# SwiGLU gate and up projections by seven block products in a two-layer encoder kernel

## The chip, the core and the metric

The kernel runs on one core of a Trainium2 chip, in one launch. The metric is the device time in microseconds. TensorE (PE) multiplies, VectorE (DVE) and ScalarE (ACT) do the elementwise work, GpSimd (POOL) a few sums, and SyncE (SP) issues nearly all transfers.

## The reference

Two layers; each has a SwiGLU, a mixer with three branches, and a second SwiGLU. Only the SwiGLUs' inner products change here. All data are float32; T = 512 tokens, D = 1024, F = 2816.

```python
def swiglu(h, w_gate, w_up, w_down):
    return (jax.nn.silu(h @ w_gate) * (h @ w_up)) @ w_down

c_act = jax.nn.silu(c)
for l in range(DEPTH):                       # 2
    mod = (c_act @ w_ada[l] + b_ada[l]).reshape(B, N_MOD, D_MODEL)       # 9 rows of 1024
    h = modulate(rms_norm(x, norm_gain[l, 0]), mod[:, 0], mod[:, 1])
    x = x + 0.5 * mod[:, 2][:, None, :] * swiglu(h, ffn_w_gate[l, 0], ffn_w_up[l, 0], ffn_w_down[l, 0])
    h = modulate(rms_norm(x, norm_gain[l, 1]), mod[:, 3], mod[:, 4])
    x = x + mod[:, 5][:, None, :] * hybrid_mixer(h, ...)
    h = modulate(rms_norm(x, norm_gain[l, 2]), mod[:, 6], mod[:, 7])
    x = x + 0.5 * mod[:, 8][:, None, :] * swiglu(h, ffn_w_gate[l, 1], ffn_w_up[l, 1], ffn_w_down[l, 1])
```

## The kernel before

Activations lie transposed, features on partitions and the 512 tokens along the columns. Every float32 product is made of three matmuls (`triple`, L117): an operand is split into a high part, rounded to fp32r, and a low part, the rest; hi x hi, hi x lo and lo x hi are added up in PSUM. The normalised input of a sub-layer is kept as `hhi` and `hlo`, eight blocks of 128 features by 512 tokens each. `pe` (L85) counts TensorE's work, in matmuls of 512 columns; `later` puts a piece of work behind a given count, and `poll` in `triple` runs what is due.

A weight chunk comes through `wchunk` (L243): a transfer of 512 KB into `raw` (two buffers), a cast on ScalarE to `whi` (L268), a subtraction on VectorE to `wlo` (L270), three buffers each. `wchunk` also fetches rows of w_ada: inside a SwiGLU, one per chunk (`MOD_RATE`), through `mod_pop` and `mod_step` (L191), which loads 512 KB into a `v2` buffer and makes the dot product with silu(c) on VectorE (L197). `mod_need` runs those rows at once that must be there by a given point.

A SwiGLU (`Ffn.run`, L461) goes in two parts, of 12 and 10 tiles of 128 hidden features. In each part, gate and up of one tile are made by eight triples each (`unit`, L447) into two `mm` banks; `act` (L452) makes silu on ScalarE, the product on VectorE in an SBUF tile `t2`, and the split into a block `b`. Then `k_outer` (L374) multiplies the part's tiles by w_down, in two halves of 512 output features: chunks of two tiles each, four accumulators of the `acc` tag, the last two chunks held back so that the accumulators end one after another. `residual_tail` (L416) adds each to x on VectorE (L420). The last half of a SwiGLU is done in two column halves of 256 tokens, so that the next norm can begin. The first tiles of a SwiGLU follow the norm in column halves too (L472 to L489); the very first SwiGLU has a start of its own (`start`, L523), which does three tiles of gate and up as the inputs arrive.

PSUM has two tags of four banks, `acc` and `mm`. SBUF tags that matter: `b` (17 blocks of 4 KB a partition), `v2` (4), `raw` (2), `whi` and `wlo` (3 each), `ptb` (2), `pta` (1), `strip` (2), `ssum` (1). The order of instructions on each engine is settled when the program is built, mainly by the order in the source; on the chip each engine takes its own in order.

Of the kernel before, what the change touches and what calls it, by code (L numbers as in the profile page):

```python
# [40 lines left out]
def encoder_kernel(tc, xT, c, w_ada, b_ada, gains, w_gate, w_up, w_down, w_qkv, w_f, w_ubg,  # L41
# [75 lines left out]
    def triple(o, lh, ll, rh, rl, start, stop):  # L117
        poll()
        mm(o, lh, rh, start=start, stop=False)  # L119
        mm(o, lh, rl, start=False, stop=False)  # L120
        mm(o, ll, rh, start=False, stop=stop)  # L121
        pe[0] += 3.0 * max(o.shape[-1], 256) / T
# [103 lines left out]
    MOD_RATE = 1.0  # L226
# [16 lines left out]
    def wchunk(src, shape, side=True, spare=None, lo_eng=None):  # L243
# [3 lines left out]
        if quiet[0] > 0:  # L247
            quiet[0] -= 1
            if quiet[0] == 0:
                gate.clear()  # L250
        elif side and in_ffn[0] and mod_tag[0] == "v2":
            mod_credit[0] += MOD_RATE
            while mod_credit[0] >= 1.0:
                mod_credit[0] -= 1.0
                mod_pop()
        raw = st([P] + list(shape), F32, *(("b", NB) if spare else ("raw", NRAW)))
# [37 lines left out]
    class Norm:  # L294


        def __init__(self, l, s, xtag):
# [5 lines left out]
            self.pieces = [[], []]  # L303

# [39 lines left out]
        def back_start(self, hs, bank):  # L344
# [9 lines left out]
            def piece(d):  # L354
# [8 lines left out]
                last["norm"] = v_ins.ins  # L363

# [9 lines left out]
    def k_outer(chunk_src, nch, lhs_rhs, before_last=None):  # L374
# [3 lines left out]
        if before_last is None:  # L378
            parts, nheld = [(None, slice(0, T), [acc() for _ in range(4)])], 2
# [14 lines left out]
        for c in range(nch):  # L394
# [34 lines left out]
    STEP = 3  # L429


    class Ffn:
# [19 lines left out]
        def act(self, n, pg, pu):  # L452
            sg = t1(T)
            nc.scalar.activation(sg, pg, AF.Silu)
            pr = t2(T)
            nc.vector.tensor_tensor(pr, pu, sg, op=ALU.mult)  # L456
            a = blk("b")
            split_to(a[:, 0, :], a[:, 1, :], pr)
            return a

        def run(self, nxt):  # L461
# [3 lines left out]
            for part, (f0, nf) in enumerate(((0, 12), (12, 10))):  # L465
                acts = []
                n = 0
                if part == 0 and self.norm is None:
                    acts = self.start()
                    n = 3  # L470
                elif part == 0:
                    g0, u0, g1 = self.pre  # L472
                    pg, pu, pg1 = mmt(), mmt(), mmt()
# [10 lines left out]
                    u1 = self.gate_up(1, 1)  # L484
# [4 lines left out]
                    n = 2  # L489
# [601 lines left out]
```

## Time and profile before

| | |
|---|---|
| time, three runs | 2480.24 us median, 2478.81 to 2480.90 |
| span of the profiled execution | 2478.9 us (its time is told by this span alone) |
| TensorE busy, matmuls | 2425.1 us (98%), 11898 |
| VectorE busy | 1372.2 us (55%) |
| ScalarE busy | 979.9 us (40%) |
| GpSimd busy | 340.5 us (14%) |
| transfers | 320.02 MB, 129 GB/s on average |
| the four SwiGLUs, about | 15 to 388, 888 to 1240, 1240 to 1628, 2128 to 2479 us |

In the profile's rows, L12 is line 12 of the kernel; PE is TensorE's matmuls and PEld its weight loads. A group's row has its count, its busy time in us and the mean of one in ns, then the idle time of its engine just before it and what ended that. A tile's or line's row has minimum, median and maximum in ns. A timeline's row begins with start and duration in us. A window's row has for each engine the busy time and, in brackets, the instructions; then the granted clock of TensorE, the share of the transfer engines and GB/s. Matmuls overlap, so the step from one start to the next tells what one costs.

### The profile page before, as it was taken

The page shows a single profiled execution, that of the slowest core. Times are in us where ns is not written, and L with a number is a line of the kernel's source. Part 1 is how long each engine was busy: PE and PEld are TensorE (multiplying, and loading weights), DVE is VectorE, ACT ScalarE, POOL GpSimd, SP SyncE. Part 2 cuts the span into 40 slices and gives each one's busy share as a digit, 9 for nine tenths or more (in the row PEclk, how much of TensorE's full clock was granted, in tenths as well). Part 3 has the DMA queues.
Part 4 walks back from the last instruction along what each step waited for, and adds up shares of the span by engine and source line. Part 5 has one row for each costly group of instructions (what it writes and reads, how often), then busy time and mean ns, then how long its engine had stood idle before and what let it go on. Part 6 is the DMA issues. An engine that isn't in the chain of part 4 may idle for free. (4 is left out here: it accounts for less than half of the span.)

```text
span 2478.9 us, 30855 instructions
## 1 busy us (share of the span) xinstructions
PE 2425.1 (98%) x11898; PEld 2030.1 (82%) x11898; DVE 1372.2 (55%) x2474; ACT 979.9 (40%) x1634; POOL 340.5 (14%) x327
## 2 busy tenths in 40 slices
PE   7999999999999999999999999999899999999999
PEld 5888888777788898888898888977778888888888
DVE  8655536788753365555365533377787434533332
ACT  5322235676532342222343223366765334432221
POOL 2000002343322200000000000124332322000000
PEclk9999999999999999999999999999999999999999
DMA  7655542222323435555335533322233233223322
GB/s 270 222 198 187 195 136 86 85 73 93 109 90 111 136 110 189 185 204 184 123 109 197 187 119 94 128 92 90 62 107 100 92 119 128 77 94 97 99 94 94
DMA packets 116263, 320.02 MB, mean 129 GB/s; under 512 B 11122, under 2 KB 13298, under 8 KB 116116
## 3 DMA queue, kind: packets, MB, share of 16 engines
q1 hardware_dynamic: 114962, 313.86, 37.9%
q0 software_dynamic: 1152, 4.19, 0.4%
q8 instruction: 93, 1.52, 0.3%
q14 instruction: 54, 0.44, 0.1%
q10 hardware_dynamic: 2, 0.00, 0.0%
HBM read 311.64 MB, written 6.38 MB: 128 GB/s over the span
## 5 line engine op out<-in xcount | busy, mean ns | idle before, releaser
L268 ACT CAST whi<-raw 128x1024 fp32r<-128x1024 f32 (+1 forms) x395 | 411.8, 1045 | 1077.3 <-PE acc L120 412.0
L270 DVE TENSOR_TENSOR wlo<-raw,whi 128x1024 fp32r<-128x1024 f32 x339 | 418.7, 1238 | 516.4 <-ACT whi L268 504.3
L121 PE MATMUL mm<-hhi,wlo 128*128 128x512 f32 x1304 | 507.4, 389 | 0.4 <-DVE wlo L270 0.4
L119 PE MATMUL mm<-hhi,whi 128*128 128x512 f32 x1304 | 507.6, 389 | 0.0
L120 PE MATMUL mm<-hlo,whi 128*128 128x512 f32 x1304 | 507.3, 389 | 0.0
L119 PE MATMUL acc<-b,whi 128*128 128x512 f32 (+1 forms) x960 | 355.9, 371 | 0.0
L121 PE MATMUL acc<-b,wlo 128*128 128x512 f32 (+1 forms) x960 | 353.5, 368 | 0.0
L120 PE MATMUL acc<-b,whi 128*128 128x512 f32 (+1 forms) x960 | 353.4, 368 | 0.0
L121 PEld LDWEIGHTS mm<-hhi,wlo 128*128 128x128 f32 x1304 | 244.8, 188 | 51.4 <-DVE wlo L270 0.9
L119 PEld LDWEIGHTS mm<-hhi,whi 128*128 128x128 f32 x1304 | 245.1, 188 | 50.9
L120 PEld LDWEIGHTS mm<-hlo,whi 128*128 128x128 f32 x1304 | 244.8, 188 | 50.8
L197 DVE CUSTOM_DVE_ANT_0 v<-v,b,badac 128x1024 f32<-128x1024 f32 x144 | 189.2, 1316 | 37.0 <-DMA v<-in_w_ada_dram 36.6
L121 PEld LDWEIGHTS acc<-b,wlo 128*128 128x128 f32 x960 | 181.0, 189 | 29.7
L120 PEld LDWEIGHTS acc<-b,whi 128*128 128x128 f32 x960 | 181.1, 189 | 29.3 <-DVE b L371 0.3
L119 PEld LDWEIGHTS acc<-b,whi 128*128 128x128 f32 x960 | 181.0, 189 | 28.8
L119 PE MATMUL acc<-hhi,whi 128*128 128x512 f32 x480 | 192.3, 402 | 1.7 <-ACT hhi L558 1.7
L121 PE MATMUL acc<-hhi,wlo 128*128 128x512 f32 x480 | 189.7, 395 | 0.6 <-POOL wlo L270 0.5
L120 PE MATMUL acc<-hlo,whi 128*128 128x512 f32 x480 | 188.9, 394 | 1.0 <-DVE hlo L561 1.0
L456 DVE TENSOR_TENSOR t<-mm,t 128x512 f32<-128x512 f32 x86 | 59.4, 691 | 202.7 <-PE mm L121 201.6
L270 POOL TENSOR_TENSOR wlo<-raw,whi 128x1024 fp32r<-128x1024 f32 (+1 forms) x56 | 132.9, 2376 | 170.9 <-ACT whi L268 136.4
L119 PE MATMUL acc<-whi,hhi 128*128 128x512 f32 x336 | 138.3, 412 | 4.9 <-ACT t L648 3.7
L120 PE MATMUL acc<-wlo,hhi 128*128 128x512 f32 x336 | 132.3, 394 | 0.0
(231 smaller groups left out, 3416.8 us busy)
## 6 DMA issues: line engine op xcount, KB each, us to landing
v<-in_w_ada_dram SPq DMA_DIRECT2D x144, 512.0 KB, 4.6
raw<-in_w_down_dram SPq DMA_DIRECT2D x88, 512.0 KB, 3.7
raw<-in_w_up_dram SPq DMA_DIRECT2D x82, 512.0 KB, 3.5
raw<-in_w_gate_dram SPq DMA_DIRECT2D x79, 512.0 KB, 3.6
raw<-in_w_ubg_dram SPq DMA_DIRECT2D x56, 512.0 KB, 3.5
raw<-in_w_qkv_dram SPq DMA_DIRECT2D x42, 512.0 KB, 3.8
raw<-in_w_branch_dram SPq DMA_DIRECT2D x24, 512.0 KB, 3.7
raw<-in_w_out_dram SPq DMA_DIRECT2D x16, 512.0 KB, 3.7
```

Source lines behind the costliest of these rows:

```text
L119: mm(o, lh, rh, start=start, stop=False)
L120: mm(o, lh, rl, start=False, stop=False)
L121: mm(o, ll, rh, start=False, stop=stop)
L197: dot = nc.vector.tensor_tensor_reduce(out=raw, in0=raw, in1=silc[0], scale=1.0, scalar=badac[:, l, j, d:d + 1], op0=ALU.mult, op1=ALU.add ...
L268: nc.scalar.copy(hi, raw)
L270: lo_eng.tensor_tensor(lo, raw, hi.bitcast(F32), op=ALU.subtract)
L456: nc.vector.tensor_tensor(pr, pu, sg, op=ALU.mult)
```

## The change

Two tiles of gate, or of up, are now made together. The weight pair is a 2 x 2 block matrix (two tiles of 128 features by two halves of the 1024 inputs), h another (two halves of the inputs by two halves of the tokens), and the four result blocks come from seven block products and not eight (Winograd's form). Each block product is 4 triples of 256 columns. Four sums of weight blocks per pair (`pair_weights`) and eight sums of h blocks per SwiGLU (`block_sums`) are made on GpSimd, and then split in high and low parts as weights are. Four intermediate results per pair are copied out of PSUM by ScalarE (`kept`), and VectorE adds them to the rest (`put`); two of the products are accumulated onto a bank that has been copied out.

In the first SwiGLU the tiles from 6 on (up from 4), in the others from 4 on (up from 2) are made this way. The up results and the product with silu stay in PSUM (`product`). A pair's sums and splits are given out in four steps among the products of the pair before (`steps`), or, behind w_down, at counts of `pe` (`then`). A SwiGLU goes in parts of 6, 6, 4 and 6 tiles; w_down's first half uses `acc` and its second `mm`. Pairs take no `wchunk`, so rows of w_ada are fetched by w_down's chunks alone (1.6 each) and by those few tiles that are made as before; and now also in the mixer (1.5 a chunk), between the second attention and the last merge.

```diff
-    MOD_RATE = 1.0
+    MOD_RATE, MIX_RATE = 1.6, 1.5
-        elif side and in_ffn[0] and mod_tag[0] == "v2":
-            mod_credit[0] += MOD_RATE
...
+        elif side and mod_tag[0] == "v2":
+            side_work(MOD_RATE if in_ffn[0] else MIX_RATE)
@@ Norm.back_start, piece
+                self.made[hs] += 1
+                if self.made == [KD, KD] and self.on_all is not None:
+                    self.on_all()
@@ k_outer
-            parts, nheld = [(None, slice(0, T), [acc() for _ in range(4)])], 2
+            parts, nheld = [(None, slice(0, T), [(bank or acc)() for _ in range(4)])], 2
+        if then is not None:
+            then()
+    PARTS = (6, 6, 4, 6)
@@ Ffn
-            pr = t2(T)
-            nc.vector.tensor_tensor(pr, pu, sg, op=ALU.mult)
+        def product(self, pu, sg):
+            nc.vector.tensor_tensor(pu, pu, sg, op=ALU.mult)
             a = blk("b")
-            split_to(a[:, 0, :], a[:, 1, :], pr)
+            split_to(a[:, 0, :], a[:, 1, :], pu)
+        def block_sums(self, norm):
...
+            else:
+                shift = {n: None for n in (1, 2, 3, 4)}
+                xa = []
+                for i in range(4):
+                    t = blk("b", F32)
+                    nc.gpsimd.tensor_tensor(t, hhi[:, 2 * i:2 * i + 2, :].bitcast(F32),
+                                            hlo[:, 2 * i:2 * i + 2, :].bitcast(F32), op=ALU.add)
+                    xa.append(t)
...
+            hi[3], lo[3] = hhi[:, 0:4, two], hlo[:, 0:4, two]
...
+            op = nc.gpsimd.tensor_tensor
+            for i in range(2):
+                op(src[3][i], src[3][i], src[1][i], op=ALU.subtract)
...
+            for n in (1, 2, 4):
+                split(n)
+            self.third = lambda: split(3)
+        def pair_weights(self, which, n):
+            src = (w_gate, w_up)[which][self.l, self.s]
+            shape = [P, 2, 4, P]
+            if which == 1:
+                d = [(st(shape, F32R, "whi", 3), st(shape, F32R, "wlo", 3)) for _ in range(3)]
+                e = st(shape, F32R, "pta", 1)
...
+            else:
...
+            r = [st(shape, F32, *(("raw", NRAW) if which else ("b", NB))) for _ in range(2)]
+            for i in range(2):
+                last["dma"] = nc.sync.dma_start(r[i].rearrange("p a k c -> p (a k) c"), src[n + i]).ins
+            r3 = st(shape, F32, "v2", 4)
+            s3 = st([P, 4, P], F32, "ssum", 1)
+            a11, a12, a21, a22 = r[0][:, 0], r[0][:, 1], r[1][:, 0], r[1][:, 1]
+            g = nc.gpsimd.tensor_tensor
+            def sums():
+                split_to(*d[0], r[0])
+                g(s3, a11, a21, op=ALU.subtract)
+                g(a21, a21, a22, op=ALU.add)
+                g(r3[:, 0], a21, a11, op=ALU.subtract)
+                g(r3[:, 1], a12, r3[:, 0], op=ALU.subtract)
+            steps = [sums, lambda: split_to(*d[1], r[1]), lambda: split_to(*d[2], r3), lambda: split_to(*e, s3)]
...
+        def pair(self, which, w, put, steps=()):
+            bank = mmt if which else acc
...
+            def prod(o, a, b, start, stop):
+                wh, wl = w[a]
+                for k in range(4):
...
+                    triple(o[:, :HALF], wh[:, k, :], wl[:, k, :], rh, rl, start and k == 0, stop and k == 3,
+                           onto=not start)
...
+            def kept(o, where):
+                nc.scalar.copy(where, o[:, :HALF])
+                return where
+            x = bank()
+            prod(x, "a11", (0, h1), True, True)
+            c1 = t2(T)
+            a = kept(x, c1[:, :HALF])
+            step()
+            y = bank()
+            prod(y, "a12", (4, h1), True, True)
+            put(0, h1, y, a)
+            v = bank()
+            prod(v, "s1", 1, True, True)
+            e = kept(v, c1[:, HALF:])
+            step()
+            prod(x, "s2", 2, False, True)
+            c2 = t2(T)
+            b = kept(x, c2[:, :HALF])
+            step()
+            z = bank()
+            prod(z, "a22", 4, True, True)
+            prod(v, "s4", (4, h2), False, True)
+            put(0, h2, v, b)
+            step()
+            if self.third is not None:
+                self.third()
+                self.third = None
+            prod(x, "s3", 3, False, True)
+            c = kept(x, c2[:, HALF:])
+            put(1, h1, z, c)
+            put(1, h2, x, e)
+        def gate_up_pair(self, n, more):
+            up, steps = self.pair_weights(1, n)
+            g = blk("v2", F32)
+            def put_gate(f, cols, p, q):
+                nc.vector.tensor_tensor(g[:, f, cols], p[:, :HALF], q, op=ALU.add)
+                if cols.stop == T:
+                    nc.scalar.activation(g[:, f, :], g[:, f, :], AF.Silu)
+            self.pair(0, self.ready, put_gate, steps)
+            self.ready, steps = self.next_pair(n + 2, more)
+            return self.up_pair(up, g, steps)
+        def gates(self, n, bank, ws):
...
+        def up_pair(self, up, g, steps):
...
+                nc.vector.tensor_tensor(u[:, cols], p[:, :HALF], q, op=ALU.add)
+                if cols.stop == T:
+                    acts.append(self.product(u, g[:, f, :]))
+            self.pair(1, up, put_up, steps)
@@ Ffn.run
-            for part, (f0, nf) in enumerate(((0, 12), (12, 10))):
+            for part, nf in enumerate(PARTS):
                 if part == 0 and self.norm is None:
                     acts = self.start()
+                    self.block_sums(None)
...
                 elif part == 0:
+                    self.norm.on_all = lambda: self.block_sums(self.norm)
...
                 while n < nf:
-                    g = self.gate_up(0, f0 + n)
-                    u = self.gate_up(1, f0 + n)
-                    pg, pu = mmt(), mmt()
-                    self.unit(pg, g)
-                    self.unit(pu, u)
-                    acts.append(self.act(n, pg, pu))
-                    n += 1
+                    acts += self.gate_up_pair(f0 + n, n + 2 < nf)
+                    n += 2
...
+                    elif c0 > 0:
+                        def then(n=f0 + nf):
+                            self.ready, steps = self.next_pair(n, not last)
+                            for i, z in enumerate(steps):
+                                later(8 * i, z)
@@ Mixer
-            mod_need(self.l, 5 if self.l + 1 < L else 8)
+            mod_need(self.l, 5)
@@ Mixer.run, behind the second attention
-            if l + 1 < L:
-                silc[0] = st([P, D], F32, "b", NB)
-                nc.sync.dma_start(silc[0], sil_dram.broadcast_to([P, D]))
+            silc[0] = st([P, D], F32, "b", NB)
+            nc.sync.dma_start(silc[0], sil_dram.broadcast_to([P, D]))
+            mod_tag[0] = "v2"
...
+            mod_tag[0] = "raw"
+            mod_need(l, 8)
             mb = merge_units(l, 1, yb, put_b)
```

More of the change, by code (lines that the diff above doesn't have):

```diff
@@ L461, in run, with next_pair @@
+        def next_pair(self, n, more):
+            return self.pair_weights(0, n) if more else (None, ())
         def run(self, nxt):
@@ L506, in ops @@
                                 acts[kt][:, 0, :], acts[kt][:, 1, :])
-                    last = part == 1
                     if last and c0 == 0 and nxt is not None:
```

119 lines of the change are left out of this document (104 added, 15 removed).

## The prediction

> **What bounds the kernel now.** I read the page's busy shares first, then a table of windows with one SwiGLU in each, then TensorE's waits inside the first of them.
>
> ```profile
> span 2478.9 us, 30855 instructions
> PE 2425.1 (98%) x11898; PEld 2030.1 (82%) x11898; DVE 1372.2 (55%) x2474; ACT 979.9 (40%) x1634; POOL 340.5 (14%) x327
> core 0: us, PE busy (x) PEld busy (x) DVE busy (x) ACT busy (x) POOL busy (x), PEclk, DMA share, GB/s
> 25.00:60.00 35.00, 33.56 (x143) 26.86 (x142) 32.80 (x46) 20.78 (x32) 13.48 (x6) 1.00 0.79 274
> 61.00:388.00 327.00, 327.00 (x1558) 275.72 (x1557) 181.38 (x272) 95.79 (x125) 10.46 (x11) 1.00 0.52 181
> 700.00:800.00 100.00, 100.00 (x442) 82.66 (x441) 38.12 (x46) 30.23 (x40) 28.84 (x27) 1.00 0.30 97
> 888.00:1240.00 352.00, 352.00 (x1698) 297.66 (x1697) 194.64 (x294) 106.29 (x139) 6.36 (x5) 1.00 0.49 171
> 2128.00:2470.00 342.00, 342.00 (x1615) 287.81 (x1614) 115.78 (x123) 89.29 (x107) 0.00 (x0) 1.00 0.31 99
> PE mm L121 <- DVE wlo L270: 0.4, 1, 0.4
> ```
>
> TensorE is busy in every microsecond of the SwiGLU windows, at a granted clock of 1.00, and the only wait there (last line, window 60 to 390) is 0.4 us. VectorE is busy 55% of such a window (181.38 of 327) and GpSimd almost never. So TensorE alone sets the time, and work taken from it counts in full as long as nobody else becomes late.
>
> What a matmul costs is its pitch, not its duration, since durations overlap. The timeline of TensorE gives the pitch: between the first two rows below lie 45 matmuls of 512 columns, between the last two 51 of 256.
>
> ```profile
> 299.62 0.39 PE L119 MATMUL mm<-hhi,whi 128*128 128x512 f32 x1
> 309.82 0.39 PE L119 MATMUL mm<-hhi,whi 128*128 128x512 f32 x1
> 358.78 0.28 PE L119 MATMUL mm<-b,whi 128*128 128x256 f32 x1
> 364.90 0.28 PE L119 MATMUL mm<-b,whi 128*128 128x256 f32 x1
> ```
>
> That is 10.20 / 45 = 0.2267 us for 512 columns and 6.12 / 51 = 0.120 us for 256. Two halves cost 0.240, 6% more than the whole, so each matmul carries about 13 ns that do not shrink with its columns.
>
> **TensorE's part of the change.** Two tiles of one weight matrix took 2 x 8 x 3 = 48 matmuls of 512 columns: 48 x 0.2267 = 10.88 us. By seven block products they take 7 x 4 x 3 = 84 of 256 columns: 84 x 0.120 = 10.08 us. A product of seven in eight saves 12.5% of the columns, but the fixed part takes back nearly half: 0.80 us a pair. The first SwiGLU computes tiles 6 to 21 so for gate and up and tiles 4, 5 for up alone, 8 x 2 + 1 = 17 pairs; the other three start at tile 4, with up alone for 2 and 3, 9 x 2 + 1 = 19. Together 17 + 3 x 19 = 74 pairs, and 74 x 0.80 = **59 us less** for TensorE. No other matmul changes.
>
> The Trainium skill (TensorE: Matmul & The Clock Gate, "Wait — 56ns, not 53.3ns?") gives the pitch as columns at 2.4 GHz plus a fixed 2.5 ns; by it a pair would save 48 x 215.8 - 84 x 109.2 ns, an estimated 1.19 us, and the sum would gain 88 instead of 59. The rows above have about 13 ns where the page has 2.5, so I go by the rows.
>
> **What the other engines get.** Rows by form, and the same line's spread:
>
> ```profile
> L268 ACT CAST whi<-raw 128x1024 fp32r<-128x1024 f32 x387 | 405.2, 1050 | 1075.3 <-PE acc L120 412.0 <-PE mm L120 362.1 <-issue 250.9
> L270 DVE TENSOR_TENSOR wlo<-raw,whi 128x1024 fp32r<-128x1024 f32 x339 | 418.7, 1238 | 516.4 <-ACT whi L268 504.3
> L357 DVE TENSOR_TENSOR v<-mm,v 128x256 f32<-128x256 f32 x40 | 14.8, 416 | 1.6 <-PE mm L351 1.6
> L820 ACT COPY t<-mm 64x256 f32<-64x256 f32 x64 | 23.5, 368 | 14.6 <-PE mm L817 7.7 <-issue 5.3
> L454 ACT ACTIVATE t<-mm 128x512 f32<-128x512 f32 x86 | 51.0, 594 | 2.1 <-PE mm L121 2.0
> L456 DVE TENSOR_TENSOR t<-mm,t 128x512 f32<-128x512 f32 x86 | 59.4, 691 | 202.7 <-PE mm L121 201.6 <-ACT t L454 1.0
> L370 ACT CAST b<-t 128x512 fp32r<-128x512 f32 x88 | 54.9, 625 | 2.3 <-DVE t L456 2.2
> L371 DVE TENSOR_TENSOR b<-t,b 128x512 fp32r<-128x512 f32 x88 | 60.1, 684 | 2.8 <-ACT b L370 2.8
> L420 DVE SCALAR_TENSOR_TENSOR xv<-acc,modc,xv 128x512 f32<-128x512 f32 x56 | 41.9, 749 | 58.2 <-PE acc L121 58.2
> L197 DVE CUSTOM_DVE_ANT_0 v<-v,b,badac 128x1024 f32<-128x1024 f32 x144 | 189.2, 1316 | 37.0 <-DMA v<-in_w_ada_dram 36.6
> L860 POOL TENSOR_TENSOR strip<-strip x12: 1039/1040/1286, 701.5 to 1941.4; 128x512 f32<-128x512 f32 x12
> L971 POOL TENSOR_TENSOR xv<-xv,t x32: 1285/1292/2372, 723.0 to 2068.4; 128x512 f32<-128x512 f32 x32
> ```
>
> One pair of one weight: weight splits of 3.5 x 1024 columns instead of 2 (two block rows, the pair r3, half a tile s3), four results kept by ScalarE, four adds from PSUM by VectorE, four block sums of 512 columns by GpSimd. Gate and up of two tiles, 20.16 us of TensorE:
>
> - ScalarE: 7 x 1.05 + 8 x 0.368 + 2 x 0.594 + 2 x 0.625 = 12.7 us. Covered.
> - VectorE: 7 x 1.238 + 8 x 0.416 + 2 x (0.691 + 0.684) = 8.7 + 3.3 + 2.75 = 14.7 us. Covered by itself.
> - GpSimd: 8 x 1.04 to 8 x 1.29 = 8.3 to 10.3 us. No row has this sum on these tiles; the two nearest rows are the bounds, and I take 10, since L971 too reads two tiles.
>
> The catch is that the last two do not run side by side. Timelines of VectorE and of GpSimd around 1885 us:
>
> ```profile
> 1881.31 0.42 DVE L371 TENSOR_TENSOR b<-t,b 64x256 fp32r<-64x256 f32 x1 [0.47 <-ACT b L370]
> 1884.03 2.57 POOL L270 TENSOR_TENSOR wlo<-raw,whi 128x1024 fp32r<-128x1024 f32 x1
> 1885.32 1.36 DVE L782 TENSOR_SCALAR t<-t,rs 128x128 f32<-128x128 f32 x1
> 1886.98 2.39 POOL L270 TENSOR_TENSOR wlo<-raw,whi 128x1024 fp32r<-128x1024 f32 x1
> 1888.00 0.42 DVE L775 CUSTOM_DVE_ANT_0 t<-mm,strip 128x256 f32<-128x256 f32 x1
> 1888.47 1.19 DVE L371 TENSOR_TENSOR b<-t,b 64x256 fp32r<-64x256 f32 x1
> ```
>
> L371 reads two SBUF tiles and takes 0.42 us with GpSimd idle, but 1.19 with GpSimd at work: it ends at 1889.66, just after GpSimd's operation does (1889.37). L782 (1.36 us, to 1886.68) likewise ends with the GpSimd operation before (1886.60). L775, with one input in PSUM, takes its 0.42 through the same GpSimd operation. So the 8.7 us of weight splits (two SBUF inputs) and GpSimd's 10 exclude each other; the adds and the products, whose first operand is in PSUM, do not. Keeping the silu product in PSUM moves its low part (0.684) to the free side. The excluding work is 18.7 of 20.16 us. How long VectorE stands blocked, B, lies between 0 (all of GpSimd's time falls on VectorE's idle or PSUM work) and 10 (none does). TensorE keeps the lead while 14.7 + B stays below 20.16, that is B below 5.4. If GpSimd's time falls on VectorE's work as it comes, 8.7 / 14.7 of it meets a split, B = 5.9, a little beyond; but VectorE's queue has gaps, and the weights of a pair are made a whole pair (10 us) ahead. I take a loss of 0.07 us a pair, 5 us in all.
>
> **Where stalls are likely.**
> - *Sums of h.* Each SwiGLU now makes eight GpSimd sums (8 x 1.29 = 10 us) and three splits of 1024 columns before its first pair. In the later three they follow the second half of the norm and have its tile units for cover (half of three units, one whole, two gates, about 25 us); VectorE has in that time norm pieces, five weight splits, two products, some five rows of w_ada and the sums: some 26 us of its own and blocked time on top. Between 0 and 10 us each, I take 3. In the first SwiGLU GpSimd also adds hhi and hlo (four sums of 1024, 2.4 each as in the rows at 1884 and 1886): 20 us plus the first up sums against 22 us of cover, while six to eight rows of w_ada are still due there: 0 to 20, I take 8. Together 17.
> - *Part of four tiles.* With two chunks of w_down, tile 3's product is needed 9 matmuls (2.0 us) after the pair's last one, and the chain behind it is copy 0.37, two adds 0.83, product 0.69, cast 0.63, low part 0.68 = 3.2 us. At least 1.2 us, at most that plus one weight split and one w_ada row queued ahead (2.5); I take 1.6, four times: 6. In parts of six the product is needed 6.8 us later, so covered.
> - *PSUM banks.* x and v are accumulated on after ScalarE's copy; two products (2.88 us) lie between, against 0.368 and one cast of 1.05 ahead. Nothing, unless a cast at the head of ScalarE's queue waits for a late GpSimd sum, which is the B case.
> - *Rows of w_ada.* They leave the gate and up tiles and go 1.6 to a w_down chunk (24 matmuls, 5.44 us): VectorE 1.24 + 1.6 x 1.4 = 3.5 us, and traffic 2.6 x 0.52 MB in 5.44 us = 250 GB/s, under the 274 of 25 to 60 us. Their SP issues now stand before w_down's and no longer between gate's and up's. In three of four parts VectorE is nearly full there (chunks 21, eight residual adds 6.0, the next pair's splits 4.3, together 31 of 32.6 us), relieved by the last up pair, which has no splits beside it. 24 rows go to the mixer, where VectorE is 38% busy (700 to 800): nothing. If that cover fails, a late split costs TensorE 1 to 2 us at each of 16 seams; I take nothing, and keep 0 to 25 for the range.
> - *More residual adds* (64 x 0.749 = 48 us of VectorE), POOL's queue (its norm sums come in the last part, where no pair is prepared) and silc's second load: covered.
>
> **Sum.** -59 + 5 + 17 + 6 = -31 us on the profiled 2478.9: 2448. The median of the runs is 1.3 above that span, so **2449 us**.
>
> **The rivals.**
> - *All hidden.* The norm's cover holds and the priorities keep needed splits first. For it: no wait at all in the SwiGLUs today and weights made a pair ahead. Against: VectorE has 15% of slack left where it had 45%. 2480 - 59 + 6 = 2427.
> - *VectorE and GpSimd become the bound (slower).* Place: the pair stage. Price: B. It decides from 14.7 + B = 21.76, today's time for the four tile halves of gate and up: B = 7.0 of GpSimd's 8.3 to 10. With B = 8.3 an iteration takes 23.0, and 37 of them (74 pairs) lose 1.24 each, +46, with the 23 us of other stalls +69: 2549. With B just past 7.0 and the same stalls, 2503. For it: the 1.19 us row. Against: VectorE's splits and GpSimd's sums for one pair come in a fixed order with a pair's lead, and a third of VectorE's work is free to run beside. The Trainium skill (SBUF — State Buffer, "Who interferes with whom") says that a VectorE instruction with two SBUF inputs and a GpSimd one that reads SBUF exclude each other, the later waiting for the whole of the earlier; the rows at 1888 us agree.
> - *Given back at the seams (no change).* Beside the 28 us of losses above, each of the 16 seams costs 2 us: -59 + 28 + 32 = +1: 2481. For it: VectorE's 31 of 32.6 us there. Against: a late w_ada row holds nobody but the splits behind it.
> - *Half the columns at half the pitch.* Were the 13 ns an effect of the residual stage and not of the matmul, a pair would cost 84 x 0.1133 = 9.52 and save 1.36: 74 x 1.36 = 101, 2480 - 101 + 28 = 2407. The Trainium skill's page named above (TensorE: Matmul & The Clock Gate, same section) leans this way. Against: the same 0.12 stands in every 256-column stretch.
>
> **How the numbers follow.** The runs lie within 2.1 us, so 5 us (0.2%) is what can be told from nothing. Chances: the forecast 0.47, all hidden 0.20, half pitch 0.02, given back 0.12, VectorE bound 0.19. Faster: 0.47 + 0.20 + 0.02 = 0.69. No change: 0.12, and 0.01 of VectorE bound, where its loss meets all other cover: 0.13. Slower: 0.18. The forecast's own range is 2432 to 2470. The range reaches down to 2424, so that it holds "all hidden", and up to 2492, through "given back" and the mild end of VectorE bound; left out are half pitch and the rest of VectorE bound, some 0.17.
>
> **What would show it.** TensorE's matmuls rise by 74 x 36 = 2664 to about 14560. The 256-column pitch in the pairs stays 0.12. VectorE's busy time rises from 1372 by 74 x (1.5 x 1.238 + 4 x 0.416) = 261, by 48 for residual adds and about 20 for the sums of h, to 1700, and by blocked time to 1800 to 1900; its split L270 goes from a mean of 1238 ns to some 1500. GpSimd rises by 74 x 4 x 1.04 to 1.29 and about 50 to 700 to 770. TensorE's busy time falls by 59, and its waits inside the SwiGLUs, nothing now, add up to about 28 us, most of them right before a SwiGLU's first pair and at the four-tile parts. I am wrong if waits on a GpSimd sum or a split stand inside ordinary pairs (VectorE bound), or if waits at the starts and seams sum to over 55 us.

## The result and the profile after

The changed kernel takes 2547.89 us (median of four, 2545.70 to 2550.13) against 2480.21: ratio 1.0277 (1.0264 to 1.0290), 2.8% slower, where I had forecast 2449, 1.3% faster. The profiled execution has a span of 2543.9 us, 65 more than before.

The head of the page, and then one row of windows in a stretch with a head and the first pairs of the third SwiGLU (columns as in the prediction):

```profile
span 2543.9 us, 37563 instructions
PE 2403.5 (94%) x14370; PEld 2111.4 (83%) x14370; DVE 1815.6 (71%) x3029; ACT 1213.8 (48%) x2122; POOL 940.5 (37%) x659
```

```profile
1300.00:1400.00 100.00, 88.67 (x517) 77.19 (x516) 78.23 (x88) 41.94 (x67) 42.67 (x27) 0.95 0.39 132
```

Before, TensorE hardly stood still in a SwiGLU; now it is busy 88.67 of 100 us, in a stretch where VectorE has 78.23 and GpSimd 42.67. No engine is full. TensorE's longest groups of waits (us in total, times, longest):

```profile
PE acc L119 <- ACT whi L271: 28.1, 7, 8.9
PE mm L119 <- ACT t L582: 20.0, 15, 2.2
PE acc L121 <- DVE wlo L273: 14.0, 5, 5.3
PE mm L1010 <- DVE t L998: 7.5, 7, 2.3
PE acc L119 <- ACT t L582: 6.3, 5, 2.4
PE acc L119 <- ACT b L378: 6.2, 5, 2.3
PE mm L121 <- DVE wlo L273: 5.8, 5, 3.2
```

L271 and L273 are the cast and the low part of an ordinary weight chunk: waits at the head of a SwiGLU and in the mixer. L582 is `kept`, ScalarE's copy of a pair's product out of PSUM: waits inside pairs. What ScalarE itself waits for shows the next link:

```profile
ACT whi L378 <- POOL v L552: 67.2, 28, 3.4
ACT v L378 <- POOL v L552: 62.3, 27, 3.4
```

55 times ScalarE stands with a weight cast at the head of its queue until GpSimd's fourth block sum (L552) is there, 129.5 us in all; a copy for TensorE may stand behind it. Grouped by form, the sums and the splits beside them (count, busy, mean ns):

```profile
L379 DVE TENSOR_TENSOR wlo<-raw,whi 128x1024 fp32r<-128x1024 f32 x78 | 134.4, 1725 | 55.6 <-ACT whi L378 55.2
L549 POOL TENSOR_TENSOR ssum<-b,b 128x512 f32<-128x512 f32 x35 | 59.1, 1688 | 482.5 <-DMA b<-in_w_gate_dram 435.4
L550 POOL TENSOR_TENSOR raw<-raw 128x512 f32<-128x512 f32 x39 | 68.1, 1746 | 3.1
```

A split took 1238 ns before and takes 1725; a sum of 512 columns, 1.04 to 1.29 us in the old rows, takes 1.76 on the mean of all 296 (shortest 1.27). The timelines show why (start, duration):

```profile
1437.91 2.16 POOL L550 TENSOR_TENSOR raw<-raw 128x512 f32<-128x512 f32 x1
1438.84 4.55 DVE L379 TENSOR_TENSOR wlo<-raw,whi 128x1024 fp32r<-128x1024 f32 x2
1440.15 2.16 POOL L551 TENSOR_TENSOR v<-raw,raw 128x512 f32<-128x512 f32 x1
1442.38 2.16 POOL L552 TENSOR_TENSOR v<-raw,v 128x512 f32<-128x512 f32 x1
```

The two engines take turns: two splits in 4.55 us, a sum every 2.24 us, nearly one split (1.22 alone) and one sum (1.27, the shortest) end to end. A sum that meets a split lasts 2.16 us in place of 1.27, and the split about 2.27 in place of 1.22. How TensorE comes to stand, some 250 us earlier, seen on GpSimd, ScalarE and TensorE:

```profile
1190.53 2.13 POOL L552 TENSOR_TENSOR v<-raw,v 128x512 f32<-128x512 f32 x1
1192.69 1.04 ACT L378 CAST whi<-v 128x1024 fp32r<-128x1024 f32 x1 [2.86 <-POOL v L552]
1193.64 0.37 ACT L582 COPY t<-acc 128x256 f32<-128x256 f32 x1
1194.06 0.39 PE L119 MATMUL acc<-b,v 128*128 128x256 f32 x1 [2.40 <-ACT t L582]
```

The cast of the pair of sums waits 2.86 us for the last sum; the copy that TensorE needs is next in ScalarE's queue; TensorE stands for 2.40 us.

To see where the 65 us lie, the trace was cut at the first matmuls of each stage (the triples of each stage are counted from the code; by this cut the SwiGLUs before run from 23 to 388, 888 to 1251, 1251 to 1615 and 2113 to 2475 us, and the bounds given ahead were rough). "Over" is a stage's time above its matmuls at 0.2267 and 0.120 us. The head of the first SwiGLU counts from its fourth tile, since the three before it follow the inputs. The mixers are given as spans.

| us over the matmuls | before | after |
|---|---|---|
| heads (tiles before the first pair), four | 2.3 | 51.4 |
| first up pairs | – | 6.0 |
| pairs (before: all other tiles) | 0.6 | 32.4 |
| w_down | 2.6 | 21.1 |
| the two mixers, span | 998.1 | 1021.0 |

The matmuls themselves fell by 62.0 us; the rows of the table rose by 128. That is +66 beside the spans' +65.

One head, that of the last SwiGLU, on ScalarE, VectorE and TensorE:

```profile
2200.03 0.63 ACT L378 CAST b<-b 128x512 fp32r<-128x512 f32 x1 [4.41 <-POOL b L501]
2201.84 4.34 DVE L516 SCALAR_TENSOR_TENSOR b<-b,modc,b 128x256 fp32r<-128x256 f32 x3
2203.62 1.99 ACT L271 CAST whi<-v 128x1024 fp32r<-128x1024 f32 x2
2210.71 0.80 PE L121 MATMUL acc<-hhi,wlo 128*128 128x512 f32 x1 [5.26 <-DVE wlo L273]
...
2212.16 0.63 PE L121 MATMUL acc<-hhi,wlo 128*128 128x512 f32 x1
2212.58 0.63 PE L119 MATMUL acc<-hhi,whi 128*128 128x512 f32 x1
```

The splits of h sums (L378, L515, L516) wait for GpSimd's sums (L501 to L505), and the weight chunk of the next gate tile (L271, and its low part) is queued behind them. After the stall the matmuls go at a step of 0.42 us (2212.16 to 2212.58), where 0.2267 was normal: the granted clock is 0.5 there. The mean clock says how much of that there is:

```profile
core 0: 2543.9 us, clock 0.985
```

A loss of 0.015 at half clock is 0.030 x 2544 = 76 us at half speed (before: 0.998, 10 us). About 85 matmuls of 512 and 46 of 256 columns go at the long step: 85 x 0.20 + 46 x 0.09 = some 21 us (before: 13, some 3 us), so that about 18 of the 128 us are this.

In the first mixer, around its longest stall: the same stretch of the mixer before and after, then VectorE, GpSimd, ScalarE and TensorE after:

```profile
697.00:717.00 20.00, 20.00 (x90) 16.48 (x89) 9.19 (x16) 7.65 (x11) 11.11 (x18) 1.00 0.27 93
716.00:736.00 20.00, 14.64 (x61) 11.73 (x60) 19.05 (x32) 5.91 (x9) 10.82 (x14) 0.87 0.80 250
```

```profile
726.50 2.06 DVE L197 CUSTOM_DVE_ANT_0 v<-v,b,badac 128x1024 f32<-128x1024 f32 x1
727.55 1.90 POOL L1076 TENSOR_TENSOR strip<-strip 128x512 f32<-128x512 f32 x1
732.40 0.62 ACT L378 CAST ptb<-ssum 128x512 fp32r<-128x512 f32 x1 [5.75 <-DVE apre L206]
732.93 1.04 ACT L271 CAST whi<-raw 128x1024 fp32r<-128x1024 f32 x1
734.02 0.79 PE L119 MATMUL acc<-hhi,whi 128*128 128x512 f32 x1 [5.36 <-ACT whi L271]
```

VectorE, busy for 9.19 of 20 us there before, is now full (19.05 us). Eight dot products of w_ada's rows take 11.7 us of that; five run at 1.27 us and three, beside the pooling sums of GpSimd (L1076), at 2.05. The cast of a pooled block waits for VectorE, the next weight cast stands behind it, and TensorE 5.36 us behind that.

### The profile page after: what moved, and what is told of

The parts are those of the page before. It is cut to its first block, busy times and chain, and to the rows that moved or that the text cites. A ratio compares the mean times of both kernels' runs of the same rounds, so it can differ in the third digit from the quotient of the medians.

```text
span 2543.9 us, 37563 instructions
## 1 busy us (share of the span) xinstructions
PE 2403.5 (94%) x14370; PEld 2111.4 (83%) x14370; DVE 1815.6 (71%) x3029; ACT 1213.8 (48%) x2122; POOL 940.5 (37%) x659
## 5 line engine op out<-in xcount | busy, mean ns | idle before, releaser
L271 ACT CAST whi<-raw 128x1024 fp32r<-128x1024 f32 (+1 forms) x241 | 250.2, 1043 | 274.4 <-PE acc L120 174.0
L273 DVE TENSOR_TENSOR wlo<-raw,whi 128x1024 fp32r<-128x1024 f32 x185 | 245.4, 1330 | 141.2 <-ACT whi L271 139.9
L119 PE MATMUL mm<-b,whi 128*128 128x256 f32 (+1 forms) x852 | 270.2, 317 | 10.7 <-ACT t L582 10.5
L119 PE MATMUL acc<-b,whi 128*128 128x512 f32 (+1 forms) x704 | 264.1, 378 | 8.4 <-ACT b L378 6.2
L121 PE MATMUL mm<-b,wlo 128*128 128x256 f32 (+1 forms) x852 | 270.0, 317 | 2.1 <-DVE wlo L273 2.0
L120 PE MATMUL mm<-b,whi 128*128 128x256 f32 (+1 forms) x852 | 268.9, 316 | 0.0
L120 PE MATMUL acc<-b,whi 128*128 128x512 f32 (+1 forms) x704 | 262.7, 373 | 2.3 <-DVE b L379 2.2
L121 PE MATMUL acc<-b,wlo 128*128 128x512 f32 (+1 forms) x704 | 261.5, 372 | 0.0
L273 POOL TENSOR_TENSOR wlo<-raw,whi 128x1024 fp32r<-128x1024 f32 (+1 forms) x56 | 133.3, 2383 | 169.2 <-ACT whi L271 122.2
L119 PEld LDWEIGHTS mm<-b,whi 128*128 128x128 f32 x852 | 162.7, 191 | 23.0 <-ACT t L582 13.1
L121 PEld LDWEIGHTS mm<-b,wlo 128*128 128x128 f32 x852 | 162.7, 191 | 14.3 <-DVE wlo L273 4.1
L379 DVE TENSOR_TENSOR wlo<-raw,whi 128x1024 fp32r<-128x1024 f32 x78 | 134.4, 1725 | 55.6 <-ACT whi L378 55.2
L120 PEld LDWEIGHTS mm<-b,whi 128*128 128x128 f32 x852 | 162.7, 191 | 10.2
L119 PE MATMUL mm<-hhi,whi 128*128 128x256 f32 (+1 forms) x524 | 155.9, 298 | 9.7 <-ACT t L582 9.5
L119 PEld LDWEIGHTS acc<-b,whi 128*128 128x128 f32 x704 | 133.2, 190 | 32.9 <-ACT b L378 9.3
L121 PE MATMUL mm<-hhi,wlo 128*128 128x256 f32 (+1 forms) x524 | 155.3, 296 | 3.8 <-DVE wlo L273 3.8
L120 PEld LDWEIGHTS acc<-b,whi 128*128 128x128 f32 x704 | 133.7, 190 | 26.2 <-DVE b L379 5.0
```

The lines of the kernel that those rows point to most:

```text
L119: mm(o, lh, rh, start=start, stop=False, skip_group_check=onto)
L120: mm(o, lh, rl, start=False, stop=False, skip_group_check=onto)
L121: mm(o, ll, rh, start=False, stop=stop, skip_group_check=onto)
L271: nc.scalar.copy(hi, raw)
L273: lo_eng.tensor_tensor(lo, raw, hi.bitcast(F32), op=ALU.subtract)
L379: nc.vector.tensor_tensor(lo, src, hi.bitcast(F32), op=ALU.subtract)
```

## The experiments

Theory: GpSimd's sums and VectorE's low parts shut each other out, and what that delays holds up ScalarE's queue and so TensorE; the rows of w_ada in the mixer cost something by themselves. Rival one: the sums and splits of h at the heads are the fault, by their place. Rival two: only the order in ScalarE's queue is at fault, not the readings of GpSimd. Differences between two kernels are taken from their ratios to the kernel before, times 2480 us. The stages of all of them, as in the table above (us over the matmuls; the mixers' span), are those of the one profiled execution, which lies up to 6 us off the median:

| | time, ratio (95%) | heads | first up | pairs | w_down | mixers |
|---|---|---|---|---|---|---|
| after | 2547.89, 1.0277 (1.0264–1.0290) | 51.4 | 6.0 | 32.4 | 21.1 | 1021.0 |
| e1_heads | 2540.46, 1.0255 (1.0240–1.0270) | 11.7 | 33.9 | 40.5 | 20.6 | 1018.0 |
| e2_order | 2530.42, 1.0213 (1.0197–1.0228) | 52.0 | 6.9 | −4.8 | 43.8 | 1017.5 |
| e3_nosums | 2482.48, 1.0016 (1.0006–1.0025) | 36.8 | 0.0 | −4.3 | 19.0 | 1020.6 |
| e6_aside | 2566.01, 1.0354 (1.0337–1.0371) | 54.6 | 1.2 | 55.1 | 24.2 | 1017.6 |
| e4_nomix | 2520.65, 1.0176 (1.0152–1.0199) | 53.2 | 4.2 | 29.2 | 21.5 | 995.7 |
| e7_dvesums | 2484.60, 1.0016 (1.0006–1.0025) | 39.8 | 0.4 | −4.8 | 18.8 | 1021.4 |
| e8_nosums_h | 2454.26, 0.9896 (0.9881–0.9911) | 8.8 | 0.0 | −4.8 | 14.0 | 1017.2 |
| e9_dve_order | 2480.37, 1.0003 (0.9993–1.0012) | 15.0 | 0.0 | −4.8 | 34.8 | 1018.5 |
| e10_memset | 2481.75, 1.0014 (1.0005–1.0023) | 29.0 | 6.1 | −4.2 | 12.6 | 1020.5 |
| e11_dve_late | 2455.24, 0.9909 (0.9894–0.9924) | 15.1 | 0.1 | −4.8 | 11.9 | 1020.9 |
| e12_mix | 2465.04, 0.9945 (0.9928–0.9962) | 11.5 | 7.3 | −4.5 | 23.1 | 1018.3 |
| e13_rows | 2500.35, 1.0088 (1.0070–1.0106) | 2.3 | – | 0.6 | 2.6 | 1017.0 |

(−4.8 is the floor of pairs: the step of 256 columns there is 0.7% under the 0.120 used.) Five times lie outside what the theory at hand had given: e1 (2500 to 2515; the rival's 2538 to 2550 held), e4 (2525 to 2532), e6 (above both theories), e7 (2490 to 2520) and e11 (2462 to 2470).

**e1_heads.** The splits of h sums are issued later, behind the loads of the next chunks.

```diff
-            for n in (1, 2, 4):
-                split(n)
+            def late():
+                for n in (1, 2, 4):
+                    split(n)
+            self.late = late
...
-                    up, g = self.gates(4, acc, [self.gate_up(0, 4 + f) for f in range(2)])
+                    ws = [self.gate_up(0, 4 + f) for f in range(2)]
+                    self.late()
+                    up, g = self.gates(4, acc, ws)
...
```

> Changed kernel, but ScalarE's and VectorE's splits of the sums of h are written behind the tiles that are made as before, so that on ScalarE the casts of those tiles' weights no longer stand behind casts that wait for GpSimd's sums. Same instructions. Order theory (queues in order behind GpSimd's sums): the stretch before each SwiGLU's first pair falls from 45 to 48 us to about 35, in the first SwiGLU from 51 to about 44; time 2548 - 40 = 2500 to 2515. VectorE-bound theory (weight splits and GpSimd's sums fill VectorE's time): the work is the same, so the time moves under 10 us: 2538 to 2550.

The heads lose 40 us of stalls, the first up pairs and the pairs take 36 of them back; 5 us are gained, and the two intervals overlap. TensorE's waits show where they went, to copies that now stand behind late splits:

```profile
PE mm L119 <- ACT t L584: 33.7, 18, 6.1
PE mm L121 <- DVE wlo L379: 12.5, 4, 4.3
```

The place in the order was not the cause at the heads: rival one fell, as long as the sums stay on GpSimd.

**e2_order.** In a pair, each step's casts are held back until the copy before them has been issued.

```diff
             def step():
                 if steps:
-                    steps.pop(0)()
+                    with tc.issue_after(copied[0]):
+                        steps.pop(0)()
...
-                nc.scalar.copy(where, o[:, :HALF])
+                copied[0] = nc.scalar.copy(where, o[:, :HALF]).ins
```

> Changed kernel, but in a pair the casts of a step may not stand ahead, on ScalarE, of the copy out of PSUM that was written before them. Same instructions. Order theory: TensorE's waits for those copies (26 us in the changed kernel) fall under 8, time about 2520 to 2530. VectorE-bound theory: the waits turn into waits for weight splits, time 2543 to 2550. If holding the casts back makes weights late, slower than 2550.

The pairs lose every wait (32.4 to −4.8): the copies did stand behind the casts, and once they go first GpSimd and VectorE keep up with TensorE inside the pairs. But w_down grows by 22.7, and 16 us are gained of 37. The held-back casts now stand ahead of the last products' casts: TensorE's waits for those (ACT b L378) rise from 6.2 to 16.9 us.

**e3_nosums and e6_aside.** The first leaves the four sums and their two buffers out and splits other blocks of the same size; the second makes four sums of the same size into those buffers, and no split reads them.

```diff
-                g(s3, a11, a21, op=ALU.subtract)
-                g(a21, a21, a22, op=ALU.add)
-                g(r3[:, 0], a21, a11, op=ALU.subtract)
-                g(r3[:, 1], a12, r3[:, 0], op=ALU.subtract)
+                g(s3, a11, a21, op=ALU.subtract)              # e6 only
+                g(r3[:, 0], a21, a22, op=ALU.add)             # e6 only
+                g(r3[:, 1], a21, a11, op=ALU.subtract)        # e6 only
+                g(r3[:, 0], a12, a22, op=ALU.subtract)        # e6 only
...
-            steps = [sums, lambda: split_to(*d[1], r[1]), lambda: split_to(*d[2], r3), lambda: split_to(*e, s3)]
+            steps = [sums, lambda: split_to(*d[1], r[1]), lambda: split_to(*d[2], r[0]), lambda: split_to(*e, a11)]
```

> Changed kernel without GpSimd's four sums of weight blocks per pair (left out: the splits take the loaded blocks instead, so results are not the reference's). Both theories: pair stages at the ideal 10.08 us a pair. Order theory: gain about 30 us in the pair stages and 10 at the seams, the SwiGLUs' heads stay at 45 to 48: 2500 to 2515. VectorE-bound theory: more, since VectorE is freed everywhere: 2480 to 2500. VectorE's weight split falls from 1725 ns (whi of pairs) to about 1240, GpSimd's busy time by 460 or more.

> As the kernel without sums, but GpSimd makes four sums of the same size per pair into scratch, for which no split waits (only their buffers). So the sharing of the read port is back and the waiting for sums is not. Order theory: within 10 us of the kernel without sums. VectorE-bound theory: within 10 us of the changed kernel, less its 50 us of heads at most.

Without sums 65 us come back. With sums whose results nobody reads, all of it is lost and 19 more: e6 less e3, same number of splits and matmuls, is 84 us. VectorE's busy time in e3, and the same group of splits in e3 and then in e6:

```profile
PE 2386.4 (96%) x14370; PEld 2102.9 (85%) x14370; DVE 1695.0 (68%) x3029; ACT 1215.1 (49%) x2122; POOL 421.8 (17%) x363
```

```profile
L379 DVE TENSOR_TENSOR wlo<-raw,whi 128x1024 fp32r<-128x1024 f32 x117 | 142.8, 1220 | 108.2 <-ACT whi L378 108.2
```

```profile
L379 DVE TENSOR_TENSOR wlo<-raw,whi 128x1024 fp32r<-128x1024 f32 x117 | 193.6, 1660 | 69.0 <-ACT whi L378 69.0
```

So no result needs to be waited for, and the loss is there. But the waiting has not gone: by the code, the sums' tile and one cast's output share the four `v2` buffers, and 11 casts stand until a fourth sum (L552) has ended. ScalarE's waits in e6, then one of them on GpSimd, ScalarE and TensorE:

```profile
ACT v L378 <- POOL v L552: 46.9, 11, 8.1
1203.39 1.26 POOL L552 TENSOR_TENSOR v<-b,b 128x512 f32<-128x512 f32 x1
1204.68 1.04 ACT L378 CAST v<-b 128x1024 fp32r<-128x1024 f32 x1 [5.67 <-POOL v L552]
1206.05 0.58 PE L119 MATMUL acc<-hhi,v 128*128 128x256 f32 x1 [3.86 <-ACT t L582]
```

The chain is that of the changed kernel: a late sum, a cast at the head of ScalarE's queue, a copy behind it, TensorE. So e6 does not part the blocking from the waiting; e10 does. Its single waits are longer than the changed kernel's (up to 8.1 us against 3.4), as are its pairs (55.1 against 32.4); that this is all of the 19 us is not shown.

**e10_memset.** GpSimd is kept at work without reading: two constants written for each sum, eight per weight pair, into the same buffers; the rest is as in e6.

```diff
+                for _ in range(2):
+                    for z in (s3, r3[:, 0], r3[:, 1], r3[:, 0]):
+                        nc.gpsimd.memset(z, 1.0)
...
```

> As the kernel with sums into scratch, but in place of each sum of 512 columns GpSimd writes two constants of 512 columns (about 0.5 us each by the row of the mixer's 64x512 write), so it is as busy and writes as much, but reads nothing (results are not the reference's). If it is the reading of GpSimd that shuts out VectorE's second operand: as the kernel without sums, 2475 to 2492. If any GpSimd work does it: as with sums into scratch, 2555 to 2570.

```profile
L379 DVE TENSOR_TENSOR wlo<-raw,whi 128x1024 fp32r<-128x1024 f32 x117 | 142.8, 1221 | 106.8 <-ACT whi L378 106.8
L551 POOL MEMSET v<- 128x512 f32 x444 | 216.7, 527 | 809.0 <-PE acc L121 345.8 <-DVE mm L470 189.8 <-DVE modc L197 169.0
```

592 memsets of 0.53 us (0.3 ms of GpSimd) leave the splits at 1221 ns and the time at e3's, though the buffers are shared as in e6. Only GpSimd's reading shuts VectorE's splits out, and rival two falls as the whole cause: the order of ScalarE's queue costs little when the work that it waits for is not blocked. The Trainium skill (SBUF — State Buffer, "Who interferes with whom") states just this: a VectorE instruction with two SBUF inputs contends with a GpSimd one that reads SBUF and not with one that only writes. These runs agree (1660 against 1221 ns).

**e7_dvesums.** The four sums go to VectorE, in the same place.

```diff
-            g = nc.gpsimd.tensor_tensor
+            g = nc.vector.tensor_tensor
```

> Changed kernel, but the four sums of weight blocks per pair are made by VectorE (0.69 us each, 296 of them, 204 us more of its own work) and not by GpSimd. Read-port theory (GpSimd's sum blocks VectorE for longer than VectorE would need to make it): faster than the changed kernel, 2490 to 2520, VectorE's split of 1024 columns back at 1.22 us. If VectorE is simply out of time, slower: 2560 and more.

```profile
PE 2388.9 (96%) x14370; PEld 2104.0 (85%) x14370; DVE 1873.4 (75%) x3325; ACT 1219.7 (49%) x2122; POOL 421.3 (17%) x363
```

```profile
L550 DVE TENSOR_TENSOR raw<-raw 128x512 f32<-128x512 f32 x39 | 26.8, 687 | 0.7
```

As fast as no sums at all (1.0016 both). VectorE makes a sum in 0.69 us where GpSimd took 1.75, and takes on 296 instructions for a busy time of 1873, only 58 us above the changed kernel's 1816, since the pairs' splits are back at 1.22 us. The price of the sums was the engine.

**e8_nosums_h.** As e3, and the eight sums of h are left out too (the splits stay, and so do the first SwiGLU's four additions of `hhi` and `hlo`).

> As the kernel without the sums of weight blocks, and without the sums of blocks of h too (left out, so results are not the reference's). Read-port theory: the heads of the SwiGLUs fall from 159 us in sum to about 130, the time from 2482 to 2450 to 2460; what is left over the kernel before minus 62 us is the mixers' and the seams'. If the heads are long from the splits of those sums and not from the sums, the time stays within 8 us of 2482.

30 us faster than e3, 28 of it at the heads: the h sums, not their splits, held the heads. 2454 is about what the changed kernel's structure gives when block sums cost nothing.

**e9_dve_order and e11_dve_late.** Both have all sums, of weights and of h, on VectorE, and the late splits of e1; e9 also holds back the casts as e2 does.

```diff
-            op = nc.gpsimd.tensor_tensor
+            op = nc.vector.tensor_tensor
...
-                    nc.gpsimd.tensor_tensor(t, hhi[:, 2 * i:2 * i + 2, :].bitcast(F32),
+                    nc.vector.tensor_tensor(t, hhi[:, 2 * i:2 * i + 2, :].bitcast(F32),
```

> Changed kernel with all block sums on VectorE (of weights and of h), with the splits of the sums of h written behind the tiles made as before, and with casts held behind the copies that TensorE waits for. The read-port and the order theory add: about 2548 - 40 - 20 - 15 = 2465 to 2490. If VectorE is out of time, the gain of the order turns into waits for splits: 2500 to 2530.

> Changed kernel with all block sums on VectorE and the splits of the sums of h written behind the tiles made as before; ScalarE's order in the pairs left as it is. If holding casts back behind copies was what lengthened w_down's stages in the run before (517 against 501 us), they come back to about 501 and the time to 2462 to 2470. If w_down's stages are long because VectorE is out of time, they stay: 2478 to 2485.

e11 does everything the change does and takes 2455.24 us: 0.9909 of the kernel before, 3 us from e8. Against e7 it has the sums of h on VectorE and the late splits, and the heads go from 39.8 to 15.1 with no loss elsewhere; which of the two did it was not separated, but in e1 late splits alone only moved the stalls. e9 is 23 us slower than e11, all in w_down (34.8 against 11.9): holding the casts back is what lengthened w_down, here and so, probably, in e2. The head of e11's page:

```profile
span 2456.3 us, 37283 instructions
PE 2373.8 (97%) x14370; PEld 2098.3 (85%) x14370; DVE 1865.4 (76%) x3361; ACT 1218.9 (50%) x2122; POOL 356.9 (15%) x327
```

**e4_nomix.** No row of w_ada is fetched in the mixers; their modulation values are constants.

```diff
+        if not in_ffn[0]:
+            nc.vector.memset(modc[:, l, j, d:d + 1], 0.5)
+            ...
+            return
```

> Changed kernel without the rows of w_ada in the mixers (left out there: those shifts, scales and gates are a constant, so results are not the reference's). If the rows that stand before weights in SP's queue cost the mixers their time, the mixers fall from 509 and 512 us to about 500 each and the time to 2525 to 2532. If the mixers are longer for another reason, nothing moves: 2543 to 2550.

The mixers fall back to 995.7, by 25 us, and the time by the same.

**e13_rows.** The other way round: the kernel before, with the mixers' rows of w_ada alone.

```diff
-    MOD_RATE = 1.0
+    MOD_RATE, MIX_RATE = 1.0, 1.5
...
-        elif side and in_ffn[0] and mod_tag[0] == "v2":
-            mod_credit[0] += MOD_RATE
+        elif side and mod_tag[0] == "v2":
+            mod_credit[0] += MOD_RATE if in_ffn[0] else MIX_RATE
...
```

> The kernel before with one part of the change alone: 24 and 11 rows of w_ada in the two mixers, as in the changed kernel (1.5 a chunk behind the second attention), and that many fewer in its SwiGLUs (at most 33, 87 and 117 rows by the end of the first, second and third). No pairs, no sums. If the rows make the mixers longer by themselves: first mixer 508 to 510, second 509 to 512 against 500 and 498, SwiGLUs unchanged, 2495 to 2505. If they do so only behind the pairs' fuller VectorE: the mixers stay within 3 us, 2476 to 2485.

22 us slower than before, with no pair in it; the mixers' span grows by 19. By the traces it has 24 and 11 rows in the two mixers, where the changed kernel has 24 in each; the first mixer takes 510.7 us (changed kernel 508.9), the second 506.3 (512.1). The first mixer's waits have a new head that the kernel before has not:

```profile
PE acc L119 <- ACT whi L270: 6.4, 1, 6.4
```

**e12_mix.** Weight sums on VectorE, h sums on GpSimd with late splits, and the mixers' rows in another place: two for each chunk in the merge of branch C, and none at the chunks of the pooling branch.

```diff
-    MOD_RATE, MIX_RATE = 1.6, 1.5
+    MOD_RATE, MIX_RATE = 1.6, 2.0
...
-        hi, lo = wchunk(w_ubg[l, g], (KD, P))
+        hi, lo = wchunk(w_ubg[l, g], (KD, P), side=False)
```

> Changed kernel with sums of weight blocks on VectorE, sums of h on GpSimd with their splits written late, and in the mixers no rows of w_ada beside the pooling branch but 2 a chunk in the merge of branch C. Heads as in the run with late splits and no lock beside, about 135 us; mixers 509 and 512 down to 500 to 505 if it was the rows' crowd beside the pools: 2445 to 2458. If the crowd only moves, the mixers stay: 2460 to 2470.

The mixers do not move (1018.3), but neither do the rows leave the pooling: branch C's chunks are worked on beside it, and between its first and last sum eight of a mixer's 24 dot products run (first mixer, 691.7 to 719.2 us), as many as in the changed kernel. So e12 does not test the crowding, and a place where those rows are free was not found. e12 is 9 us slower than e11, whose h sums are on VectorE; it loses at the first up pairs and in w_down, and which of its two differences does it was not separated.

## Why the prediction was wrong

Its terms, against what the stages show (us):

| step | forecast | measured |
|---|---|---|
| TensorE's matmuls | −59 | −62.0 |
| pair stage, B | +5 | +37.8 (6.0 + 32.4 − 0.6) |
| sums of h, at the heads | +17 | +49.1 (51.4 − 2.3) |
| parts of four tiles | +6 | +9.8, within w_down |
| seams of w_down | 0 | +8.7, the rest of w_down's 18.5 |
| rows of w_ada in the mixer | 0 | +22.9 |
| sum | −31 | +66 |

- **TensorE's part held.** 2664 matmuls more were forecast; 2664 for the pairs came, and 192 fewer because the part that is done in column halves shrank from ten tiles to six, which I had missed: 64 triples x 0.04 us = 2.6 us of gain. The step of 256 columns stayed at 0.12, so neither the rival of half pitch nor the estimate by the Trainium skill's 2.5 ns fixed cost (TensorE: Matmul & The Clock Gate) came true.
- **The step that failed first is the test for B**, "TensorE keeps the lead while 14.7 + B stays below 20.16". B itself was not far off: VectorE's busy time in e3 is 1695.0, in the changed kernel 1815.6 with the same instructions, and 120.6 us over 37 iterations is 3.3 us each, under the threshold of 5.4. A capacity was left over, as the forecast said, and e2 shows pairs without a wait. But a sum of busy times says nothing of when a result arrives. Only VectorE's blocked time had a price, GpSimd's had none: four sums, 4.2 to 5.2 us in the forecast, take 7.0 on the mean (4 x 1.76) and 9.0 in turns with splits (4 x 2.24). The cast that waits for the fourth stands at the head of ScalarE's queue, and the PSUM copies behind it. The prediction named that place ("Nothing, unless a cast at the head of ScalarE's queue waits for a late GpSimd sum") and then priced it by B. Changing the engine of the sums is worth 65 us (e7), of which the profile of e3 places 37 in the pairs, 15 at the heads, 6 in the first up pairs and 2 in w_down. The price of a sum could be read before. The forecast took 1.29 us from L971, a median; the same line grouped by form has a mean of 1751 ns, nearly the 1.76 that came:

```profile
L971 POOL TENSOR_TENSOR xv<-xv,t 128x512 f32<-128x512 f32 x32 | 56.0, 1751 | 200.2 <-DVE t L970 200.2
```

  Of its 32 executions 18 took 1.29 us and 14 took 2.32 to 2.37, each of the 14 beside a weight split on VectorE.
- **The sums of h** were mis-sized: the first head 13 for 8, the three later 36 for 9. I had 26 us of work beside 25 of cover and took 3 of 0 to 10; the splits there are longer too, and the gate tiles' own weight chunks stand behind them. e8 gives 30 us for the h sums.
- **The parts of four tiles** cost 9.8 for 6, with the blocked sums in them; with all sums on VectorE (e11) they cost 3.6.
- **"24 rows go to the mixer … nothing"** failed: 22 us by themselves (e13), 25 out of the whole (e4). The average of 38% hid that the rows arrive in bunches (19.05 of 20 us busy). TensorE's idle time in the two mixers rose from 33.7 to 49.4 us, of which 11.5 are one long stall in each. At the stall shown, GpSimd's pooling made dot products last 2.05 us; that this crowding costs the rest too is not shown.
- **Left out altogether:** the half clock that came with each stall of over 3 us, some 18 us inside the terms above. A loss priced by its wait alone is too small.
- **The rival "VectorE and GpSimd become the bound"** gave 2549 and the time is 2547.89. Its mechanism, the exclusion, is shown by e6, e7 and e10. Its composition is only partly right: it put +46 net of TensorE's gain on the pairs and 23 elsewhere, where the pairs stand at 38 − 62 = −24 net and the other places at +90; and no engine became the bound by its busy time. That its number lies within 1 us is luck. "Given back at the seams" had a true place, w_down, with 18.5 of the 38 us that it put there (32, and 6 of the four-tile parts).
- The marks: VectorE's 1800 to 1900 busy held (1815.6), split means of 1500 were 1352 to 1725, GpSimd's 700 to 770 became 940.5 because a blocked sum counts as busy, and the sign for being wrong, waits on a sum inside ordinary pairs, is what stands there; so does the other sign, with 49.1 at the heads and 18.5 in w_down against its 55.

What stays open: how much of e6's extra 19 us its longer waits make up; and which part of the rows' work (VectorE's time, its meeting with the pooling, the transfers or their place in SyncE's queue) costs the mixer its time.

## What to carry to other kernels

Do not give GpSimd elementwise work that reads SBUF while VectorE makes two-input splits from SBUF: here the two ran nearly end to end, and VectorE does the same sum in 0.69 us against 1.75, so 65 us were to be had by changing one word. Read the mean and the spread of a row, not its median: two groups of durations in one row are two conditions. A sum of busy times under the bound does not show that nothing waits; follow one result through the queues it passes, and ask what stands behind it at the head of each. A change that moves side work should be tried with that work alone (e13): a third of this loss had nothing to do with the seven products.

## What the runs showed of the hardware

- GpSimd writing constants does not slow VectorE's two-input instructions (1221 ns beside 592 memsets), GpSimd reading does (1352 to 1725 ns by group); in lock step a split of 1.22 and a sum of 1.27 us make a period of 2.24.
- The profile counts the blocked time as busy on both engines: GpSimd's 74 x 4 sums show some 520 us of busy time (940.5 less e3's 421.8) for some 376 us of work at 1.27, their shortest.
- With each of the seven stalls of over 3 us after the kernel's start, TensorE's granted clock fell to 0.5, for 3.4, 6.8 or 10.2 us, and with some, not all, of those of 1.2 to 2.4 us; the mean clock went from 0.998 to 0.985, and a 512-column step from 0.2267 to 0.42 us.
